# RWKV inverses and chunk steps on eight heads at a time in place of four, scores' B and K rows in separate PSUM banks, bonus product in DRAM

## Chip, cores, metric

One core of one Trainium2 chip. The metric is the device time of one execution in microseconds, median over runs. Engines: TensorE (PE), VectorE (DVE), ScalarE (ACT), SyncE (SP, which here only issues DMAs).

## What is computed

A decoder trunk of four residual layers, batch 1, 256 tokens, width 2048, all in float32: RWKV-7, dilated attention, pooling, RWKV-7. Each layer norms, projects in, mixes, gates and projects out. The change touches the two RWKV layers (32 heads of 64), whose mixer is this recurrence:

```python
def step(state, inp):                      # per head, state (64 x 64)
    r_t, w_t, k_t, v_t, a_t, b_t = inp
    sa = jnp.einsum('bhij,bhj->bhi', state, a_t)
    state = (state * w_t[:, :, None, :] + sa[..., None] * b_t[:, :, None, :]
             + v_t[..., None] * k_t[:, :, None, :])
    y_t = jnp.einsum('bhij,bhj->bhi', state, r_t)
    return state, y_t
...
y = _head_group_norm(y, lnx_w, lnx_b)
bonus = jnp.sum(heads(r * k) * r_k, axis=-1, keepdims=True) * vf
y = (y + bonus.reshape(B, S, D)) * jax.nn.silu(g)
```

## The kernel before

**Weights stream.** Every projection is `linear` (L244): 512 KB chunks of weights come by DMA on SP into `raw` (four buffers, `weights` L189), ScalarE casts them to `whi` (L196), VectorE makes the rest `wlo` (L197), and 24 matmuls `lin` per chunk (L287, 128x128 weights by 256 tokens; three products xhi·whi, xlo·whi, xhi·wlo) use it.

**The scan.** The recurrence runs in chunks of 64 tokens (four of them, `NC_`). `heads` (L675) is a generator, called eight times a layer with four heads each (`pr`; q counts two column tiles, hh the two heads in one). Its stages:

- A and S: the decays, then scores `sc` (L750): rows B and K (`BK`) against A and R (`AR`), per chunk and head 128x128; masked copies of them are `NT`, `MR` and parts of `AR`. `BT` is the transpose of `BK` (`tps` L769).
- D: the inverse of a triangular 64x64 matrix for each head and chunk. `NT` goes to DRAM and back as 16x16 blocks `Nb` on 64 partitions; 15 steps of a product and an add on VectorE (`tmp` L792, `px` L795) invert the blocks; then matmuls on 32x32 tiles (`q` L818, `zp` L834, `pp` L843) put them together to `P`.
- C: a chunk step, four times in order: `xps` (L869) from the state `SV`, its copy `X` (ACT), `ups` (L876), its copies `UV` (DVE L879, ACT L880), `sps` (L884) with the state update on VectorE (an add L887 and a product L889 per half), and the output `yps` (two groups, L894 and L897). The values of all four chunks are loaded into `SV` and `UV` at once.
- E: the epilogue: group norm sums `gps` (L909), bonus sums `bps`, norm, gate, and the store of z, which the layer's last projection reads.

**What sets the order.** `tick` (L200) is called by `linear` after every few lins. It holds the generators in a queue and draws from them; every `yield` gives the TensorE time and the delay that the step is planned with. The order of each engine is fixed when the program is built. Work of the scan so lies between lins of the same layer's projections: r, lower half of k and v, upper half of k and v, g.

A matmul of fp32 is recorded as two records in the profile.

Of the kernel before, what the change touches and what calls it, by code (L numbers as in the profile page):

```python
# [15 lines left out]
P = 128  # L16
# [79 lines left out]
class Trunk:  # L96
    def __init__(self, tc, ins, out, ctx, layers=(0, 1, 2, 3)):
# [22 lines left out]
        self.vcd = self.dp.tile([KT // 2, S, 2 * P], F32, name="vcd")  # L120
        self.ntd = [self.dp.tile([C, 2, 8, C], F32, name=f"ntd{i}") for i in range(2)]
        self.pxd = [self.dp.tile([16, 64, 32], F32, name=f"pxd{i}") for i in range(2)]

    def constants(self):
# [17 lines left out]
        n0, n1 = ix[("mu", 0, 0)], ix[("mu", 1, 5)] + 1  # L142
        self.omm = self.cp.tile([P, 12 * KT], F32, name="omm")
        nc.vector.tensor_scalar(self.omm, self.prm[:, n0 * KT:n1 * KT], -1.0, 1.0,
                                op0=ALU.mult, op1=ALU.add)
# [345 lines left out]
    def mix(self, l, m, k):  # L491
# [10 lines left out]
        for q in range(2):  # L502
# [4 lines left out]
            else:  # L507
                o = (l * 6 + m) * KT + k + q
# [73 lines left out]
    def rwkv(self, l, li):  # L582
        nc = self.nc
        a = self.i
        w2, srcs, have = {}, {}, (set(), set(), set(), set(), set(), set())
        win = lambda m: a["a_w_in"][l, m]
# [13 lines left out]
        def take_v(j, ps):  # L600
# [13 lines left out]
            def turn():  # L614

                vps = self.ps.tile([P, 2, 2, 2, C], F32, tag="ch", name="vps", bufs=2)
                for tt in range(2):
# [5 lines left out]
                nc.scalar.dma_start(  # L623
                    self.vcd[j // 2].rearrange("(t p) c -> p t c", p=P), vc)
# [50 lines left out]
    def heads(self, l, li, pr, w2, srcs, have):  # L675
# [6 lines left out]
        FLY = 3  # L682
# [7 lines left out]
        r = T("r", [P, 2, S], 1)  # L690
        dma(r, self.rd[j // 2])
# [26 lines left out]
        kp = T("kp", [P, 2, S], FLY)  # L718
        for q in range(2):
            nc.vector.scalar_tensor_tensor(kk[:, q], kt[:, q], self.col(("k_k", l), j + q),  # L720
                                           nrm[:, q], op0=ALU.mult, op1=ALU.mult)
            nc.scalar.activation(kp[:, q], aa[:, q], AF.Identity,
                                 scale=self.col(("k_a", l), j + q),
                                 bias=self.omka[:, l * KT + j + q:l * KT + j + q + 1])
        yield 0.9, 3.0
        nc.vector.tensor_tensor(kp, kp, kt, op=ALU.mult)
        BK = T("BK", [P, 2, NC_, 2, C], 1)
        AR = T("AR", [P, 2, 2, NC_, 2, C], FLY)
        for hh, rows in enumerate(half):
            nc.vector.scalar_tensor_tensor(AR[rows, hh, :, :, 0, :], c3(kk)[rows], -1.0,  # L730
                                           W[rows, :, :, 0:C], op0=ALU.mult, op1=ALU.mult)
            nc.vector.tensor_tensor(AR[rows, hh, :, :, 1, :], c3(r)[rows], W[rows, :, :, 1:],
                                    op=ALU.mult)
        nc.vector.tensor_tensor(aa, aa, kk, op=ALU.mult)
        nc.vector.tensor_tensor(BK[:, :, :, 0, :], c3(aa), c3(Wi), op=ALU.mult)
        nc.vector.tensor_tensor(BK[:, :, :, 1, :], c3(kp), c3(Wi), op=ALU.mult)
# [3 lines left out]
        yield 0.0, 5.0  # L740
# [3 lines left out]
        NT = T("NT", [P, 8, C], 2)  # L744
        MR = T("MR", [64, 2, 2, NC_, C], FLY)
        for q in range(2):
            scs = [self.ps.tile([P, NC_, 2, C], F32, tag="sm", name="sc", bufs=2) for _ in half]
            for c in range(NC_):
                for hh, rows in enumerate(half):
                    nc.tensor.matmul(scs[hh][:, c], BK[rows, q, c], AR[rows, hh, q, c],  # L750
                                     start=True, stop=True)
            yield 1.8, 2.0
            for hh, rows in enumerate(half):
                sc = scs[hh]
                nc.scalar.copy(NT[rows, q * NC_:(q + 1) * NC_], sc[0:64, :, 0, :])
                nc.vector.tensor_tensor(MR[:, q, hh], sc[0:64, :, 1, :],
                                        mk[0:64, C:].unsqueeze(1).broadcast_to([64, NC_, C]),
                                        op=ALU.mult)
                nc.vector.tensor_tensor(  # L759
                    AR[half[1 - hh], hh, q].rearrange("p c a t -> p c (a t)"),  # L760
                    sc[64:128].rearrange("p c a t -> p c (a t)"),
                    mk[64:128].unsqueeze(1).broadcast_to([64, NC_, 2 * C]), op=ALU.mult)
            yield 0.0, 1.0

        BT = T("BT", [P, 2, NC_, P], FLY)
        for q in range(2):
            tps = self.ps.tile([P, NC_, P], F32, tag="sm", name="tps", bufs=2)
# [3 lines left out]
            nc.scalar.copy(BT[:, q], tps)  # L771
        yield 0.9, 1.0

        yield "D", lambda: True
        ntd, pxd = self.ntd[pr % 2], self.pxd[pr % 2]
        for hh, rows in enumerate(half):
            dma(ntd[:, hh], NT[rows])
        Nb = T("Nb", [64, 16, 16], 1)
        for b in range(4):
            o = 16 * b  # L780
            dma(Nb[16 * b:16 * b + 16],
                ntd[o:o + 16, :, :, o:o + 16].rearrange("i h n t -> (h n) i t"))
        px = T("px", [64, 16, 2, 16], 1)
        nc.scalar.copy(px[:, :, 0], self.cst("eye16")[0:64].rearrange("p (i t) -> p i t", i=16))
        yield 0.0, 7.0
        tmp = T("tmp", [64, 64], 1)
        with self.tc.high_priority(PRIO_D):
            for i in range(15):
# [3 lines left out]
                nc.vector.tensor_tensor(t, px[:, 0:i + 1, 0, i:i + 1].broadcast_to([64, i + 1, w]),  # L792
                                        Nb[:, i:i + 1, i + 1:].broadcast_to([64, i + 1, w]),
# [3 lines left out]
        dma(pxd.rearrange("i p w -> p i w"), px.rearrange("p i w t -> p i (w t)"))  # L797
# [529 lines left out]
```

## Time and profile before

| | |
|---|---|
| median of 3 runs | 2279.78 us (2279.2 to 2280.67) |
| profiled execution | 2284.08 us, span 2282.3 us |
| PE busy | 2210.9 us (97%) |
| DVE busy | 1578.4 us (69%) |
| ACT busy | 1299.8 us (57%) |
| chain that ended last | PE 73%, DVE 13%, DMA 8%, ACT 3% |
| scans | 146 to 626 us (layer 0), 1690 to 2195 us (layer 3) |

The span is the time from the first instruction to the last on the core; the profiled execution's own time has what lies around it too. Records of matmuls overlap, so the distance from one start to the next tells more than the length of a record.

### The profile page before, as it was taken

What the parts mean: (1) busy time and instruction counts of PE and PEld (TensorE: products, weight loads), DVE (VectorE), ACT (ScalarE), POOL (GpSimd) and SP (SyncE); (2) the same over time, 40 slices, a digit from 0 to 9 for tenths busy, and PEclk for the clock granted to TensorE, in tenths of its full rate; (3) what the DMA queues carried; (4) which work ended last, traced back from release to release, by engine and by line L of the source; (5) the groups of instructions that cost most, each with busy time, mean ns of one, the idle gap of its engine ahead of it and who ended that gap; (6) DMA issues with size and microseconds to landing.
All of it is one profiled execution on the core that took longest, in us unless ns stands there. A gap on an engine that the chain in (4) does not pass through costs nothing.

```text
span 2282.3 us, 51163 instructions
## 1 busy us (share of the span) xinstructions
PE 2210.9 (97%) x21034; PEld 2025.7 (89%) x21034; DVE 1578.4 (69%) x2881; ACT 1299.8 (57%) x2050; POOL 4.7 (0%) x12
## 2 busy tenths in 40 slices
PE   7998999999999999999999999999998999999999
PEld 6998888888899888888899999998997888888989
DVE  7678788887556564656467675657677788787654
ACT  6557666665545454545466445546666666676542
POOL 0000000000000000000000000000000000000000
PEclk9999999999999999999999999999998999999999
DMA  7676777755576555355537556766585676665664
GB/s 267 224 265 184 231 216 211 215 178 173 195 245 201 186 185 194 129 177 184 193 122 257 172 182 220 249 219 228 175 296 181 209 232 202 193 200 171 204 217 154
DMA packets 217642, 464.16 MB, mean 203 GB/s; under 512 B 55488, under 2 KB 85824, under 8 KB 217408
## 3 DMA queue, kind: packets, MB, share of 16 engines
q1 hardware_dynamic: 199264, 432.92, 59.0%
q10 hardware_dynamic: 17504, 25.87, 3.3%
q8 instruction: 165, 2.70, 0.5%
q0 software_dynamic: 640, 2.10, 0.2%
q14 instruction: 69, 0.57, 0.1%
HBM read 410.47 MB, written 50.33 MB: 202 GB/s over the span
## 4 chain that ended last, share of the span: by engine, by line
PE 73%; DVE 13%; DMA 8%; ACT 3%; issue 2%; SPq 1%; DVEq 0%; POOL 0%; ACTq 0%; POOLq 0%
PE lin L287 44%; PE lin L321 17%; DMA hl<-hd 3%; DVE wlo L197 3%; PE u L542 1%; DVE xlo L173 1%; ACT whi L196 1%; DMA zl<-zd 1%; DVE mt L505 1%; PE z L567 1%; PE q L818 1%; PE yps L897 1%; DMA kt<-kd 1%; PE xps L869 1%; DVE AR L759 1%
## 5 line engine op out<-in xcount | busy, mean ns | idle before, releaser
L287 PE MATMUL lin<-xhi,whi 128*128 128x256 f32 x3584 | 1056.3, 295 | 12.3 <-ACT xhi L172 11.9
L197 DVE TENSOR_TENSOR wlo<-raw,whi 128x1024 fp32r<-128x1024 f32 x600 | 732.4, 1222 | 441.1 <-ACT whi L196 429.7
L287 PE MATMUL lin<-xlo,whi 128*128 128x256 f32 x3584 | 1024.8, 286 | 8.5 <-DVE xlo L173 8.5
L287 PE MATMUL lin<-xhi,wlo 128*128 128x256 f32 x3584 | 1022.0, 286 | 0.6 <-DVE wlo L197 0.6
L196 ACT CAST whi<-raw 128x1024 fp32r<-128x1024 f32 x600 | 627.6, 1048 | 572.0 <-PE lin L287 364.8
L287 PEld LDWEIGHTS lin<-xhi,whi 128*128 128x128 f32 x3584 | 689.0, 193 | 35.9 <-ACT xhi L172 15.0
L287 PEld LDWEIGHTS lin<-xlo,whi 128*128 128x128 f32 x3584 | 690.7, 193 | 20.1 <-DVE xlo L173 11.8
L287 PEld LDWEIGHTS lin<-xhi,wlo 128*128 128x128 f32 x3584 | 690.4, 193 | 5.0 <-issue 1.9
L321 PE MATMUL lin<-whi,xhi 128*128 128x512 f32 x576 | 229.5, 399 | 0.0
L321 PE MATMUL lin<-whi,xlo 128*128 128x512 f32 x576 | 224.6, 390 | 0.0
L321 PE MATMUL lin<-wlo,xhi 128*128 128x512 f32 x576 | 224.4, 390 | 0.0
L321 PEld LDWEIGHTS lin<-whi,xlo 128*128 128x128 f32 x576 | 108.1, 188 | 22.8
L321 PEld LDWEIGHTS lin<-wlo,xhi 128*128 128x128 f32 x576 | 108.3, 188 | 20.9
L321 PEld LDWEIGHTS lin<-whi,xhi 128*128 128x128 f32 x576 | 108.3, 188 | 20.7
L505 DVE SCALAR_TENSOR_TENSOR mt<-hl,prm 128x256 f32<-128x256 f32 x152 | 71.2, 477 | 28.2 <-DMA hl<-hd 27.1
L172 ACT CAST xhi<-mt 128x512 fp32r<-128x512 f32 x96 | 58.8, 616 | 43.4 <-DVE mt L505 37.0
L173 DVE TENSOR_TENSOR xlo<-mt,xhi 128x512 fp32r<-128x512 f32 x96 | 65.2, 683 | 5.3 <-ACT xhi L172 4.8
L509 ACT ACTIVATE mt<-H,omm 128x256 f32<-128x256 f32 x120 | 54.1, 501 | 20.9 <-PE u L542 11.3
L511 DVE SCALAR_TENSOR_TENSOR mt<-H,prm,mt 128x256 f32<-128x256 f32 x120 | 52.8, 480 | 15.7 <-ACT mt L509 14.1
L792 DVE TENSOR_TENSOR tmp<-px,Nb 64x15 f32<-64x15 f32 (+7 forms) x240 | 46.7, 194 | 5.3 <-DMA Nb<-ntd 0.7
L795 DVE TENSOR_TENSOR px<-px,tmp 64x15 f32<-64x15 f32 (+7 forms) x240 | 46.8, 195 | 4.5
L759 DVE TENSOR_TENSOR AR<-sc,c 64x512 f32<-64x512 f32 x64 | 44.4, 694 | 1.4
(228 smaller groups left out, 2222.8 us busy)
## 6 DMA issues: line engine op xcount, KB each, us to landing
raw<-in_a_w_in_dram SPq DMA_DIRECT2D x256, 512.0 KB, 4.1
raw<-in_b_qkv_dram SPq DMA_DIRECT2D x144, 512.0 KB, 3.3
hl<-hd SPq DMA_DIRECT2D x152, 256.0 KB, 4.5
raw<-in_a_w_out_dram SPq DMA_DIRECT2D x64, 512.0 KB, 4.3
raw<-in_c_w_in_dram SPq DMA_DIRECT2D x64, 512.0 KB, 3.3
raw<-in_c_w_out_dram SPq DMA_DIRECT2D x32, 512.0 KB, 3.8
raw<-in_b_gate_dram SPq DMA_DIRECT2D x16, 512.0 KB, 3.2
raw<-in_b_w_out_dram SPq DMA_DIRECT2D x16, 512.0 KB, 4.7
```

The source lines that it names most:

```text
L172: nc.scalar.copy(hi, src)
L173: nc.vector.tensor_tensor(lo, src, hi.bitcast(F32), op=ALU.subtract)
L196: nc.scalar.copy(whi, raw)
L197: nc.vector.tensor_tensor(wlo, raw, whi.bitcast(F32), op=ALU.subtract)
L287: nc.tensor.matmul(ps[:, m], a, b, start=(k == 0 and m == 0 and q == 0), stop=(k == kt - 1 and q == 2), skip_group_check=True)
L321: nc.tensor.matmul(ps, a[:, sl], b[:, kk], start=(k == 0 and q == 0), stop=(k == KT - 1 and q == 2))
L505: nc.vector.scalar_tensor_tensor(t[:, q], h[q][:, 1], mu, h[q][:, 0], op0=ALU.mult, op1=ALU.add)
L509: nc.scalar.activation(t[:, q], self.H[:, k + q, 1:], AF.Copy, scale=self.omm[:, o:o + 1])
L511: nc.vector.scalar_tensor_tensor(t[:, q], self.H[:, k + q, 0:S], mu, t[:, q], op0=ALU.mult, op1=ALU.add)
L759: nc.vector.tensor_tensor(AR[half[1 - hh], hh, q].rearrange("p c a t -> p c (a t)"), sc[64:128].rearrange("p c a t -> p c (a t)"), mk[64:1 ...
L792: nc.vector.tensor_tensor(t, px[:, 0:i + 1, 0, i:i + 1].broadcast_to([64, i + 1, w]), Nb[:, i:i + 1, i + 1:].broadcast_to([64, i + 1, w]), ...
L795: nc.vector.tensor_tensor(dst, dst, t, op=ALU.add)
```

## The change

Each `heads` call now ends after the scores and transposes and puts its tiles into a list, and every second call goes on into a new generator, `group`, with eight heads: inverse (`Nb`, `px`, `tmp`, `PX` on 128 partitions, 16 blocks), chunk steps and epilogue (the latter twice, for four heads each). Four groups a layer take the place of eight.

Scores: `sb` and `sk` are two banks; weights are the 64 columns of B or of K, on four different quarters of the array for (B, head 0), (B, head 1), (K, head 0), (K, head 1), so `MR` has 128 partitions. Transposes become matmuls with a 64x64 identity, into quarters.

Values: `SV` and `UV` are loaded for one chunk at a time (two buffers each, four DMAs a chunk), from a store that ScalarE's queue writes in two DMAs rather than one. The bonus product `kp` is stored to DRAM (`bd`) and loaded in the epilogue. r is loaded later, into the buffer of `kt`. `raw` has three buffers, not four. `AR`, `MR`, `BT` and `Wc` have four, not three; the vector `omm` (1 - mu) is made per layer. Flags in `st` keep one user of `BK`, `NT` and `Y` at a time, and let a `heads` call start only when the group before the last has ended its chunks.

```diff
@@ __init__, weights
-        self.vcd = self.dp.tile([KT // 2, S, 2 * P], F32, name="vcd")
+        self.bd_ = self.dp.tile([KT // 2, P, 2, S], F32, name="bd")
+        self.vcd = self.dp.tile([KT // 4, S, 2, 2, 2, C], F32, name="vcd")
-        raw = self.wp.tile([P, k, nb], F32, tag="raw", name="raw", bufs=4)
+        raw = self.wp.tile([P, k, nb], F32, tag="raw", name="raw", bufs=3)
@@ heads: four heads a call
-        kp = T("kp", [P, 2, S], FLY)
+        kp = T("kp", [P, 2, S], 1)
...
+        while st["BK"]:
+            yield 0.0, 1.0
+        st["BK"] = True
+        r = T("kt", [P, 2, S], 1)
+        dma(r, self.rd[j // 2])
...
+        dma(self.bd_[j // 2], kp)
...
-            scs = [self.ps.tile([P, NC_, 2, C], F32, tag="sm", name="sc", bufs=2) for _ in half]
+            sb, sk = (self.ps.tile([P, NC_, 2, C], F32, tag="sm", name="sc", bufs=2)
+                      for _ in range(2))
             for c in range(NC_):
                 for hh, rows in enumerate(half):
-                    nc.tensor.matmul(scs[hh][:, c], BK[rows, q, c], AR[rows, hh, q, c],
+                    nc.tensor.matmul(sb[rows, c], BK[rows, q, c, 0], AR[rows, hh, q, c],
+                                     start=True, stop=True)
+                for hh, rows in enumerate(half):
+                    nc.tensor.matmul(sk[half[1 - hh], c], BK[rows, q, c, 1], AR[rows, hh, q, c],
                                      start=True, stop=True)
...
-                nc.tensor.transpose(tps[:, c], BK[:, q, c].rearrange("p b t -> p (b t)"),
-                                    self.cst("ident"))
+                for b in range(2):
+                    for hh, rows in enumerate(half):
+                        nc.tensor.matmul(tps[hh][half[hh ^ b], q, c], BK[rows, q, c, b],
+                                         idn[rows, rows], start=True, stop=True)
...
+        st["BK"] = False
+        grp.append((AR, MR, BT, Wc))
+        if pr % 2:
+            yield from self.group(l, li, pr // 2, have, grp, st)
+
+    def group(self, l, li, gr, have, grp, st):
...
-        for n in range(8):
+        for n in range(16):
...
+        def values(c):
+            SV = T("SV", [P, 2, 2, 2, C], 2)
+            UV = T("UV", [P, 2, 2, 2, C], 2)
+            vc = vv[c * C:(c + 1) * C]
+            for hh, rows in enumerate((half[1], half[0])):
+                for t in (SV, UV):
+                    dma(flat(t[rows, hh]), flat(vc[:, hh]))
+            return SV, UV
...
-            for q, hh, rows in each:
-                nc.tensor.matmul(xps[rows, q], AR[:, hh, q, c, 0, :], SV[:, c, hh, q, :],
+            xps = bank("xps")
+            for s, q, hh, rows in each:
+                nc.tensor.matmul(xps[rows, q, s], grp[s][0][:, hh, q, c, 0, :], SV[:, hh, q, s],
                                  start=True, stop=True)
+            nxt = values(c + 1) if c < NC_ - 1 else None
...
-                    nc.vector.tensor_tensor(SV[rows, c + 1, hh], SV[rows, c, hh], sps[rows],
-                                            op=ALU.add)
-                    nc.vector.tensor_tensor(SV[rows, c + 1, hh], SV[rows, c + 1, hh],
-                                            Wc[rows, :, c:c + 1].broadcast_to([64, 2, C]),
-                                            op=ALU.mult)
+                    S_ = nxt[0][rows, hh]
+                    nc.vector.tensor_tensor(S_, SV[rows, hh], sps[rows], op=ALU.add)
+                    for s in range(2):
+                        nc.vector.tensor_tensor(
+                            S_[:, :, s], S_[:, :, s],
+                            grp[s][3][rows, :, c:c + 1].broadcast_to([64, 2, C]), op=ALU.mult)
...
+            dma(kp, self.bd_[j // 2])
```


The inverse's steps keep their form at twice the size, and `zp`, `pp`, `ups`, `sps`, `yps` follow the pattern of `xps`.

**TensorE, a score set in layer 0.** Names are out<-moving,weights and each tile's number; a row with x2 is two alike. Before:

```order
L750 MATMUL sc_4605<-AR_4369,BK_4368 128x128
L750 MATMUL sc_4606<-AR_4369,BK_4368 128x128
L750 MATMUL sc_4605<-AR_4369,BK_4368 128x128
L750 MATMUL sc_4606<-AR_4369,BK_4368 128x128
L750 MATMUL sc_4605<-AR_4369,BK_4368 128x128
L750 MATMUL sc_4606<-AR_4369,BK_4368 128x128
L750 MATMUL sc_4605<-AR_4369,BK_4368 128x128
L750 MATMUL sc_4606<-AR_4369,BK_4368 128x128
L876 MATMUL ups_4617<-X_4615,P_4558 64x64 x4
L287 MATMUL lin_4525<-xhi_3629,whi_4467 128x256
```

Of the change, at a set of the same layer (L771 is B, L774 is K; L920 is `xps`, L284 is `lin`):

```order
L284 MATMUL lin_4647<-xhi_4673,wlo_4583 128x256
L771 MATMUL sc_5053<-AR_4360,BK_4359 64x128 x2
L774 MATMUL sc_5054<-AR_4360,BK_4359 64x128 x2
L771 MATMUL sc_5053<-AR_4360,BK_4359 64x128 x2
L774 MATMUL sc_5054<-AR_4360,BK_4359 64x128 x2
L771 MATMUL sc_5053<-AR_4360,BK_4359 64x128 x2
L774 MATMUL sc_5054<-AR_4360,BK_4359 64x128 x2
L284 MATMUL lin_4647<-xhi_4770,whi_4582 128x256
L771 MATMUL sc_5053<-AR_4360,BK_4359 64x128 x2
L774 MATMUL sc_5054<-AR_4360,BK_4359 64x128 x2
L920 MATMUL xps_5159<-SV_5151,AR_2721 64x64 x4
```

Eight matmuls of 128x128 have become eight of B and eight of K, in pairs; here a lin stands among them, and `xps` of a group follows in the same run.

**TensorE, a chunk step near the end of layer 0's scan.** Before, from `sps` to the next `xps`:

```order
L884 MATMUL sps_8606<-UV_8448,BT_7331 64x64 x4
L287 MATMUL lin_8709<-xhi_8346,wlo_8482 128x256
L287 MATMUL lin_8709<-xhi_8372,whi_8481 128x256
L287 MATMUL lin_8709<-xlo_8373,whi_8481 128x256
L287 MATMUL lin_8709<-xhi_8372,wlo_8482 128x256
L287 MATMUL lin_8709<-xhi_8372,whi_8481 128x256
L894 MATMUL yps_8615<-AR_6761,SV_8449 64x64 x4
L897 MATMUL yps_8615<-MR_7089,UV_8448 64x64 x4
L287 MATMUL lin_8709<-xlo_8373,whi_8481 128x256
L287 MATMUL lin_8709<-xhi_8372,wlo_8482 128x256
L287 MATMUL lin_8709<-xhi_8372,whi_8481 128x256
L869 MATMUL xps_8625<-SV_8449,AR_6761 64x64 x4
```

Of the change (L936 `sps`, L947 and L950 `yps`):

```order
L936 MATMUL sps_8371<-UV_8293,BT_6985 64x64 x4
L936 MATMUL sps_8371<-UV_8293,BT_7459 64x64 x4
L947 MATMUL yps_8386<-AR_6033,SV_8292 64x64 x4
L947 MATMUL yps_8386<-AR_7111,SV_8292 64x64 x4
L950 MATMUL yps_8386<-MR_6718,UV_8293 64x64 x4
L950 MATMUL yps_8386<-MR_7242,UV_8293 64x64 x4
L284 MATMUL lin_8616<-xhi_8103,whi_8252 128x256
L920 MATMUL xps_8404<-SV_8309,AR_6033 64x64
L284 MATMUL lin_8616<-xlo_8104,whi_8252 128x256
L284 MATMUL lin_8616<-xhi_8103,wlo_8253 128x256
L920 MATMUL xps_8404<-SV_8309,AR_6033 64x64 x3
L920 MATMUL xps_8404<-SV_8309,AR_7111 64x64 x4
```

The step has twice the matmuls, for two sets of tiles (two numbers of `BT`, `AR`, `MR`); `sps` and `yps` stand together, and three lins lie between `yps` and the end of the next `xps`.

**VectorE, the same stretch.** Before, the state updates (L887, L889) and the copies `UV`, without the tiles' numbers:

```order
L879 COPY UV<-ups 64x128
L887 TENSOR_TENSOR SV<-SV,sps 64x128 x2
L889 TENSOR_TENSOR SV<-SV,Wc 64x128 x2
L197 TENSOR_TENSOR wlo<-raw,whi 128x1024
L925 TENSOR_TENSOR Y<-Y,gl 128x512
L173 TENSOR_TENSOR xlo<-zl,xhi 128x512 x2
L879 COPY UV<-ups 64x128
L173 TENSOR_TENSOR xlo<-zl,xhi 128x512
L197 TENSOR_TENSOR wlo<-raw,whi 128x1024
L887 TENSOR_TENSOR SV<-SV,sps 64x128 x2
L889 TENSOR_TENSOR SV<-SV,Wc 64x128 x2
```

Of the change (L940, L942, L931):

```order
L931 COPY UV<-ups 64x256
L940 TENSOR_TENSOR SV<-SV,sps 64x256 x2
L942 TENSOR_TENSOR SV<-SV,Wc 64x2x64 x4
L194 TENSOR_TENSOR wlo<-raw,whi 128x1024
L636 TENSOR_TENSOR gs<-gs,lin 128x512
L931 COPY UV<-ups 64x256
L940 TENSOR_TENSOR SV<-SV,sps 64x256 x2
L942 TENSOR_TENSOR SV<-SV,Wc 64x2x64 x4
L194 TENSOR_TENSOR wlo<-raw,whi 128x1024
L931 COPY UV<-ups 64x256
L940 TENSOR_TENSOR SV<-SV,sps 64x256 x2
L942 TENSOR_TENSOR SV<-SV,Wc 64x2x64 x4
```

An update was four operations of 128 elements a row; it is two of 256 and four of 2x64 a row (that is 128), for twice the heads, and there are half as many updates.

## Rows read from the trace of the kernel before

**Rows 1.** Windows of both scans, summed; columns: engine and its busy us.

```profile
sum 985.00, PE 942.32 PEld 834.90 DVE 766.88 ACT 642.84 POOL 0.00; mean PE 471.16 PEld 417.45 DVE 383.44 ACT 321.42 POOL 0.00
```

**Rows 2.** Same windows, `lin` alone: window, us, PE busy (count), granted clock, DMA share, GB/s.

```profile
146.00:626.00 480.00, 321.37 (x2280) 0.99 0.66 204
1690.00:2195.00 505.00, 332.32 (x2295) 0.97 0.64 201
```

**Rows 3.** TensorE timeline in layer 0: start us, us, then line, tile, shapes, records.

```profile
562.16 0.28 PE L287 MATMUL lin<-xhi,wlo 128*128 128x256 f32 x1
562.37 0.45 PE L869 MATMUL xps<-SV,AR 128*64 128x64 f32 x8
...
562.97 0.28 PE L287 MATMUL lin<-xlo,whi 128*128 128x256 f32 x1
...
565.10 0.45 PE L876 MATMUL ups<-X,P 64*64 64x64 f32 x8
...
565.70 0.28 PE L287 MATMUL lin<-xlo,whi 128*128 128x256 f32 x1
...
567.62 0.28 PE L287 MATMUL lin<-xhi,wlo 128*128 128x256 f32 x1
...
568.44 0.45 PE L897 MATMUL yps<-MR,UV 64*64 64x64 f32 x8
...
569.04 0.28 PE L287 MATMUL lin<-xlo,whi 128*128 128x256 f32 x1
569.16 0.28 PE L287 MATMUL lin<-xhi,wlo 128*128 128x256 f32 x1
```

**Rows 4.** TensorE timeline, a score set in layer 0.

```profile
178.30 0.28 PE L287 MATMUL lin<-xhi,wlo 128*128 128x256 f32 x1
178.51 1.16 PE L750 MATMUL sc<-AR,BK 64*128 64x128 f32 x16
...
179.82 0.28 PE L287 MATMUL lin<-xlo,whi 128*128 128x256 f32 x1
```

**Rows 5.** TensorE timeline, transposes and inverse in layer 0.

```profile
436.97 1.03 PE L769 MATMUL tps<-c,BK 128*128 128x128 f32 x8
...
437.96 0.28 PE L287 MATMUL lin<-xlo,whi 128*128 128x256 f32 x1
...
438.43 0.28 PE L287 MATMUL lin<-xhi,wlo 128*128 128x256 f32 x1
438.64 0.72 PE L818 MATMUL q<-Z,PX 32*32 32x32 f32 x62
...
440.11 0.28 PE L287 MATMUL lin<-xlo,whi 128*128 128x256 f32 x1
```

**Rows 6.** Groups by form, VectorE: state update and masks (busy us, mean ns; idle before).

```profile
L889 DVE TENSOR_TENSOR SV<-SV,Wc 64x128 f32<-64x128 f32 x96 | 27.4, 286 | 2.7
L887 DVE TENSOR_TENSOR SV<-SV,sps 64x128 f32<-64x128 f32 x96 | 27.3, 284 | 18.7 <-PE sps L884 16.7
L756 DVE TENSOR_TENSOR MR<-sc,c 64x256 f32<-64x256 f32 x64 | 26.5, 415 | 9.5 <-ACT NT L755 8.2
```

**Rows 7.** Page part 5: the rest of the weights, and the inverse's products.

```profile
L197 DVE TENSOR_TENSOR wlo<-raw,whi 128x1024 fp32r<-128x1024 f32 x600 | 732.4, 1222 | 441.1 <-ACT whi L196 429.7
...
L792 DVE TENSOR_TENSOR tmp<-px,Nb 64x15 f32<-64x15 f32 (+7 forms) x240 | 46.7, 194 | 5.3 <-DMA Nb<-ntd 0.7
```

**Rows 8.** Waits of TensorE: for what, us in total, times, longest us.

```profile
PE xps L869 <- DVE SV L889: 2.2, 6, 0.4
```

**Rows 9.** TensorE timeline at the end of layer 0's scan.

```profile
625.53 1.04 PE L909 MATMUL gps<-gsq,c 128*128 128x512 f32 x2
...
636.51 0.51 PE L287 MATMUL lin<-xhi,whi 128*128 128x256 f32 x2
```

**Rows 10.** Waits of SyncE's queue.

```profile
SPq L193 <- DVE wlo L197: 1109.7, 473, 8.5
```

**Rows 11.** DMA issues: tile, engine, count, KB each, median us to landing.

```profile
SV<-vcd SPq DMA_DIRECT2D x32, 128.0 KB, 3.7
```

More of the change, by code (lines that the diff above doesn't have):

```diff
@@ L827, in heads @@
         pp = prod(lambda o, n: Z[:, n], P0, 32)
-        yield 2.6, 2.0
+        yield 2.6, 2.5
         nc.vector.tensor_tensor(X0, X0, xp, op=ALU.add)
         nc.vector.tensor_tensor(P0, P0, pp, op=ALU.add)
-        zp = self.ps.tile([P, 8, 32], F32, tag="nt", name="zp", bufs=2)
-        for n in range(8):
+        zp = bank("zp")
+        for n in range(16):
             for b in (0, 64):
@@ L835, in heads @@
                                  start=True, stop=True)
[L836 to L837 removed]
+        st["NT"] = None
+        yield 1.0, 2.0
+        Z2 = T("px", [P, 16, 32], 1)
         for b in (0, 64):
             nc.scalar.copy(Z2[b + 32:b + 64], zp[b + 32:b + 64])
[L840 to L841 removed]
+        pp = bank("pp")
+        for n in range(16):
             for b in (0, 64):
@@ L844, in heads @@
                                  start=True, stop=True)
-        Pm = T("P", [P, 8, C], 2)
+        yield 1.0, 1.5
+        yield "C", lambda: (4 * gr in have[2] and 4 * gr + 2 in have[2] and not st["Y"])
+        Pm = T("P", [P, 16, C], 1)
         for o in range(2):
@@ L861, in heads @@
+        each = [(s, q, hh, rows) for s in range(2) for q in range(2)
+                for hh, rows in enumerate(half)]
+        SV, UV = values(0)
         for hh, rows in enumerate(half):
-            nc.vector.memset(SV[rows, 0, hh], 0.0)
-        Y = T("Y", [P, 2, S], 1)
-        each = [(q, hh, rows) for q in range(2) for hh, rows in enumerate(half)]
+            nc.vector.memset(SV[rows, hh], 0.0)
+        bank = lambda name: self.ps.tile([P, 2, 2, C], F32, tag="ch", name=name, bufs=2)
         for c in range(NC_):
-            xps = self.ps.tile([P, 2, C], F32, tag="ch", name="xps", bufs=2)
-            for q, hh, rows in each:
-                nc.tensor.matmul(xps[rows, q], AR[:, hh, q, c, 0, :], SV[:, c, hh, q, :],
+            xps = bank("xps")
+            for s, q, hh, rows in each:
+                nc.tensor.matmul(xps[rows, q, s], grp[s][0][:, hh, q, c, 0, :], SV[:, hh, q, s],
@@ L870, in heads @@
                                  start=True, stop=True)
-            yield 0.44, 1.3
-            X = T("X", [P, 2, C], 2)
+            nxt = values(c + 1) if c < NC_ - 1 else None
+            yield 0.5, 1.3
+            X = T("X", [P, 2, 2, C], 1)
             nc.scalar.copy(X, xps)
-            ups = self.ps.tile([P, 2, C], F32, tag="ch", name="ups", bufs=2)
-            for q, hh, rows in each:
-                nc.tensor.matmul(ups[rows, q], Pm[rows, q * NC_ + c], X[rows, q],
-                                 start=True, stop=True)
@@ L892, in heads @@
-            yps = self.ps.tile([P, 2, C], F32, tag="ch", name="yps", bufs=2)
-            for q, hh, rows in each:
-                nc.tensor.matmul(yps[rows, q], SV[:, c, hh, q, :], AR[:, hh, q, c, 1, :],
-                                 start=(q == 0), stop=False, skip_group_check=True)
-            for q, hh, rows in each:
-                nc.tensor.matmul(yps[rows, q], UV[0:64, c, hh, q, :], MR[:, q, hh, c, :],
-                                 start=False, stop=True, skip_group_check=True)
@@ L899, in heads @@
-            yield 1.21, 1.3
-            nc.scalar.copy(Y[:, :, c * C:(c + 1) * C], yps)
+            ups = bank("ups")
+            for s, q, hh, rows in each:
+                nc.tensor.matmul(ups[rows, q, s], Pm[rows, s * 8 + q * NC_ + c],
+                                 X[rows, q, s], start=True, stop=True)
+            yield 0.4, 1.6
+            nc.vector.tensor_copy(UV[0:64, 0], ups[0:64])
+            nc.scalar.copy(UV[64:128, 1], ups[64:128])
+            if nxt:
+                sps = bank("sps")
+                for s, q, hh, rows in each:
+                    nc.tensor.matmul(sps[rows, q, s], grp[s][2][:, hh, q, c],
+                                     UV[:, hh, q, s], start=True, stop=True)
+                for hh, rows in enumerate(half):
+                    S_ = nxt[0][rows, hh]
[4 more added lines that the diff above has]
+                            grp[s][3][rows, :, c:c + 1].broadcast_to([64, 2, C]), op=ALU.mult)
@@ new lines, in group @@
+            yps = bank("yps")
+            for s, q, hh, rows in each:
+                nc.tensor.matmul(yps[rows, q, s], SV[:, hh, q, s], grp[s][0][:, hh, q, c, 1, :],
+                                 start=(s == 0 and q == 0), stop=False, skip_group_check=True)
+            for s, q, hh, rows in each:
+                nc.tensor.matmul(yps[rows, q, s], UV[rows, hh, q, s], grp[s][1][rows, q, c],
+                                 start=False, stop=True, skip_group_check=True)
+            yield 1.6, 1.5
```

201 lines of the change are left out of this document (106 added, 95 removed).

## Prediction

> **What bounds the kernel now.** I read the page first (its busy shares), then the two stretches in which the changed code runs: the scans of layer 0 (146 to 626 us) and of layer 3 (1690 to 2195 us), by windows of engine time. Of their 985.0 us TensorE is busy for 942.3 and VectorE for 766.9 [rows 1]; idle time of TensorE is 42.7 us. So in both scans the time is TensorE's stream, in its own order, and VectorE is second with some room. The same windows for the tile `lin` alone count 2280 and 2295 instructions, at a granted clock of 0.99 and 0.97 (nearly all of the time the upper level, 2.4 GHz) [rows 2]. A lin that follows a lin starts 0.12 us after it (569.04 and 569.16 in [rows 3]; all plain stretches read so), so they take 4575 x 0.12 = 549 us of the 985. The other 436 us are small matmuls put between lins, and waits. Idle time is only 43 of them. What the change can save is therefore what a small matmul adds to TensorE's stream, not what it is busy for (records overlap); I read that from start to start.
>
> Between the last lin before a piece of small work and the second lin behind it lie two lin pitches, 0.24 us, and the rest was added. For the eight records of xps (four matmuls of fp32, two records each, 64 columns a record): 562.97 - 562.16 - 0.24 = 0.57 us [rows 3]. For the sixteen of sc, 128 columns each: 179.82 - 178.30 - 0.24 = 1.28 us [rows 4]. The first are 512 columns and the second 2048, so a column costs 0.71 / 1536 = 0.46 ns and what is left, 0.33 us, is paid for entering and leaving tiled matmuls once, whatever their number. I call that a **run**. The run sps, yps, yps at the end of a chunk step adds 569.04 - 567.62 - 0.24 = 1.18 us [rows 3]: 0.33 + 3 x 0.24 leaves 0.14, and in it the tile changes once, from 128*64 to 64*64. So a **change of tile inside a run** is 0.14 us. The inverse's q, 128 records of 32 columns on 32*32 tiles, adds 440.11 - 438.43 - 0.24 = 1.44 us [rows 5]; less 0.33 that is 0.27 ns a column against 0.46: the four tiles on the array's diagonal work at once, where xps and sc have two.
>
> **The change part by part.** *Fewer runs.* Columns of the inverse and of the chunk steps stay as they are, since eight heads need twice the columns of four in half as many runs. I counted runs (tiled matmuls between two lins) and changes of tile inside them in TensorE's order of the whole program: runs 274 before and 185 after, changes 124 and 53. That gives 89 x 0.33 = -29 us and 71 x 0.14 = -10 us.
>
> *Scores.* A set had 16 records of 128 columns on two row halves of the array; it now has 32 on 64*64 tiles, B and K apart. No row of before has four 64*64 tiles at once. Bounds: at the two-at-a-time price of rows 3 and 4, 4096 x 0.46 = 1.89 us a set, 0.95 more than now, times 32 sets = +30 us; at half that price, nothing. I take nothing, since in the order the four tiles of a chunk follow each other (two of B, two of K) and lie in four different quarters of the array, and q shows four tiles at work. Four of the 32 sets have their B and K rows drawn apart by the scheduler and then only pairs can meet: 4 x 0.9 = +4 us.
> The Trainium skill (TensorEngine Tiling (Array Packing), Gotcha 1: PSUM Pressure) says that different row tiles cannot access the same PSUM bank simultaneously; by it, B's two matmuls, which lie in one bank on different rows, would take turns, as would K's, and the sum would come out as the first rival's below. The trace differs: the runs ups and yps<-MR do that now, and 565.70 - 565.10 for ups is no longer than 562.97 - 562.37 for xps, 0.60 us each [rows 3].
>
> *Transposes.* A call's eight records of 128 columns run in the lins' own tile and add 437.96 - 436.97 - 0.12 = 0.87 us [rows 5], 14 us for 16 calls. Now they are 64 records of 64 columns, four at a time 4096 x 0.23 = 0.94 us, 15 us (their runs are counted above): +1. Two at a time: +15 more.
>
> *State update.* VectorE did two adds of 284 ns and two products of 286 ns, 1.14 us, between sps and the next xps; now two adds of 256 elements, for which the 415 ns of the like operation MR<-sc stands, and four products of 286 [rows 6]: 1.97 us. In 17 of the 24 chunk steps followed by another, far more lins than that stand between and hide it. In seven, at the layers' tails, two to five lins do (0.24 to 0.6 us). There yps gives 2 x 0.47 + 0.14 of cover, so 1.97 and some 0.2 for the hand-over less 1.3 to 1.7 is 0.5 to 0.9 us of waiting; a wlo of 1.22 us [rows 7] stands in VectorE's order at some of them, which makes at most 2.1. Bounds 7 x 0.5 = 3 to 7 x 2.1 = 15; I take 7 x 1.3 = 9. Now this wait is six times, 2.2 us in all [rows 8]. What is queued behind xps then is the lins of the layer's last part, so it is time on the path. Four of the eight inverses also have q, q and zp with no lin between, at the 0.3 us of such a hand-over: +1.
>
> *Tail.* The last epilogue now makes two z blocks after each other; 11 us pass from gps to the lin that reads the block (625.53 to 636.51) [rows 9], and 62 to 83 lins (7 to 10 us) stand there in the order, 76 and 83 before: +2, between 0 and 6.
>
> *VectorE's relief.* The 240 products of the inverse, at 194 ns, and its 240 adds, taken at the same, become half as many: -47 us [rows 7]. Masks (MR) halve from 64 x 415 ns: -13. The update falls from 96 x 570 ns to 24 x 1.97 us: -7 [rows 6]. That is 67 of 767 us, 9%. If TensorE's 42.7 us of waits fall by as much, -4; bounds 0 and -21 (half of them).
>
> *Edits at nothing.* One raw buffer less: the weight loads would have 2.9 us less to be ahead by, where a chunk of 24 lins takes 24 x 0.12. Of a load's waits for its buffer the typical is 1109.7 / 473 = 2.3 us on SyncE behind VectorE's wlo [rows 10], with the cast still far ahead of the lins; if that cover went, each late chunk would cost up to 2.9 us, and 20 of them 58. The bonus product's store and reload (16 of 256 KB each way), the values' store in two transfers in place of one, the later load of r and the flags lie tens of us ahead of their readers. Chunk loads: the second rival.
>
> Sum: -29 - 10 + 4 + 1 + 9 + 1 + 2 - 4 = **-26 us**. The profiled execution took 2284.1, 4.3 above the median of the runs shown, so 2258 on its scale and **2254 us** against the median. 0.2% is 4.6 us, about what a measurement here can tell from no change.
>
> **The rivals.** *Tiles in pairs (slower).* If four 64*64 tiles don't work at once, scores cost +30 and transposes +15: -26 + 45 = +19, or 2299 us; if only the scores are hit, +4, 2284. For it: no row shows four. Against it: q, and ups in one bank. The kernel is slower by over 0.2% from 0.23 + 0.23 x (26 + 4.6) / 45 = 0.39 ns a column.
>
> *Chunk loads late (slower).* SV and UV come per chunk now, 24 times behind the first, each time four transfers issued on SyncE behind weight loads that wait. A transfer lands after 3.7 us [rows 11], and the wait ahead of it is 2.3 us in the mean, 8.5 at the longest [rows 10]: 6.0 to 12.2 us. A chunk step has at least 6.7 us from its xps to the next where lins are plenty (562.37 to beyond 569.04 [rows 3]), less in the seven tail steps. It makes the kernel slower by over 0.2% from a mean wait of (26 + 4.6) / 24 = 1.3 us a load; at 2 us it is +48 - 26 = +22, 2302 us. Against it: the issue stands a whole step ahead, and a wait there is only what those two numbers leave over.
>
> *Waits halve (faster still).* Half as many inverses and chains mean half as many hand-overs: -21 in place of -4, **2237 us**. Against it: many of the 43 us belong to norms, mixes and the lora products, which stay.
>
> **How the numbers follow.** Forecast 0.66 (own range 2240 to 2270, from the bounds of update, tail and relief), waits halve 0.08, pairs 0.13 (0.01 faster, 0.04 same, 0.08 slower), late loads 0.10 (slower), something unforeseen 0.03 (0.02 the same, 0.01 slower). Faster 0.66 + 0.08 + 0.01 = 0.75, same 0.06, slower 0.19. The range runs from 2230 (below the third rival) to 2282, which leaves out the late loads and most of the pairs.
>
> **What the profile of the changed kernel would show.** Runs: xps with sixteen records adding 0.33 + 0.47 = 0.80 us from lin to lin; 1.14, twice the 0.57 of now, says that the price of a run grows with its records, and then the 29 us are not there. Scores: 32 records adding 1.3 us (four at a time) or 2.2 (pairs). Transposes: 64 records adding 1.3 or 2.2. Waits of xps for SV's products at the tails, about 9 us in all; for SV's loads, under 1. If waits of lin for wlo or whi appear in the scans, the raw buffer was not free.

## The result, and the profile after

The changed kernel takes **2317.24 us** (median) against 2280.23 for the kernel before, a ratio of 1.0157 (95% interval 1.0137 to 1.0177): slower by 37 us, where 26 us faster had been forecast. One of the four executions behind the median took 10449 us at a granted clock of 0.184; the ratio leaves it out. The profiled execution took 2314.95 us, 30.9 more than that of before.

The changed kernel's page, the rows on the span, on TensorE and on its granted clock in 40 slices:

```profile
span 2313.2 us, 53463 instructions
...
PE 2194.3 (95%) x22442; PEld 2026.7 (88%) x22442; DVE 1510.2 (65%) x2482; ACT 1257.2 (54%) x1850; POOL 4.6 (0%) x12
...
PEclk9999898989999999999999999999999999999999
```

TensorE is busy for 16.6 us less than before (2210.9) and the span is 30.9 us longer. The clock falls in the slices of the first scan. The windows of rows 1, for the changed kernel:

```profile
sum 985.00, PE 896.74 PEld 817.36 DVE 689.10 ACT 589.80 POOL 0.00; mean PE 448.37 PEld 408.68 DVE 344.55 ACT 294.90 POOL 0.00
```

and those of rows 2, `lin` alone (window, us, PE busy and count, granted clock, DMA share, GB/s):

```profile
146.00:626.00 480.00, 304.55 (x2211) 0.94 0.66 205
1690.00:2195.00 505.00, 334.53 (x2414) 0.95 0.69 214
```

VectorE did get the forecast relief (on the whole page 1510.2 us in place of 1578.4, -68; forecast -67). But TensorE is idle for 985.0 - 896.7 = 88 us in place of 43, and the granted clock is 0.94 and 0.95 in place of 0.99 and 0.97 [rows 1, 2]. The windows hold the same times, not quite the same work: the last gps of the two scans now begin at 648.5 and 2224.8 us, behind the windows' ends.

The prices of single runs, from TensorE's timeline in layer 0 (start us, us):

```profile
181.80 0.28 PE L284 MATMUL lin<-xhi,wlo 128*128 128x256 f32 x1
182.01 0.33 PE L771 MATMUL sc<-AR,BK 64*64 64x128 f32 x2
...
183.26 0.28 PE L284 MATMUL lin<-xlo,whi 128*128 128x256 f32 x1
...
311.59 0.28 PE L284 MATMUL lin<-xhi,wlo 128*128 128x256 f32 x1
311.80 0.69 PE L920 MATMUL xps<-SV,AR 128*64 128x64 f32 x16
...
312.64 0.28 PE L284 MATMUL lin<-xlo,whi 128*128 128x256 f32 x1
...
519.64 0.28 PE L284 MATMUL lin<-xhi,wlo 128*128 128x256 f32 x1
519.85 0.69 PE L936 MATMUL sps<-UV,BT 128*64 128x64 f32 x16
...
521.77 0.28 PE L284 MATMUL lin<-xlo,whi 128*128 128x256 f32 x1
```

As in the prediction, from the last lin before to the second behind, less 0.24: a set of scores adds 183.26 - 181.80 - 0.24 = 1.22 us (forecast 1.3 with four tiles at once, 2.2 in pairs), xps 312.64 - 311.59 - 0.24 = 0.81 (0.80), sps with both yps 521.77 - 519.64 - 0.24 = 1.89 (0.33 + 3 x 0.47 + 0.14 = 1.88). The price list was right to 0.1 us. The loss is in the waits of TensorE (us in total, times, longest):

```profile
PE q L860 <- issue: 44.0, 16, 4.0
PE lin L284 <- ACT xhi L169: 23.5, 15, 5.8
...
PE bps L972 <- DMA kb<-bd: 6.9, 5, 2.1
...
PE lin L284 <- DVE xlo L170: 5.8, 12, 1.3
...
PE zp L876 <- issue: 2.7, 2, 1.7
```

In the kernel before the first row was:

```profile
PE q L818 <- issue: 2.8, 3, 2.2
```

Now it is 44.0 us in 16, two in each of the eight inverses. "Issue" is time in which TensorE waited for nothing that the profile shows. Taken together, the rows of this view rose from 66.2 to 114.2 us: +41 for issue, +9 for DMAs (kb above all), -2 for everything else. One inverse in the timeline:

```profile
257.29 1.29 PE L860 MATMUL q<-PX,NT 16*32 16x32 f32 x128
...
259.65 0.43 PE L771 MATMUL sc<-AR,BK 64*64 64x128 f32 x2
261.20 0.62 PE L860 MATMUL q<-px,PX 32*32 32x32 f32 x49 [1.12 <-ACT px L867]
264.05 1.27 PE L860 MATMUL q<-px,PX 32*32 32x32 f32 x77 [2.23 <-issue]
...
269.97 1.12 PE L860 MATMUL q<-PX,px 32*32 32x32 f32 x68 [4.00 <-issue]
...
273.42 0.64 PE L876 MATMUL zp<-PX,NT 32*32 32x32 f32 x15 [1.00 <-issue]
...
276.28 0.41 PE L284 MATMUL lin<-xlo,whi 128*128 128x256 f32 x1
276.49 0.41 PE L284 MATMUL lin<-xhi,wlo 128*128 128x256 f32 x1
```

The two products q (L860, 256 records) begin at 261.20 and go on past 270; 2 x 1.11 = 2.2 us follow from the prediction's price for 128 records. They stand still twice, for 2.23 and 4.00 us, and again in zp. The lins behind run at 276.49 - 276.28 = 0.21 us each, not at 0.12. The windows say why (us, PE busy and count, granted clock, DMA share, GB/s):

```profile
258.00:262.00 4.00, 2.70 (x127) 1.00 1.03 333
262.00:266.00 4.00, 1.93 (x128) 0.72 0.80 255
266.00:270.00 4.00, 0.03 (x4) 0.50 0.91 314
270.00:274.00 4.00, 3.00 (x145) 0.50 0.46 156
274.00:278.00 4.00, 4.00 (x45) 0.58 0.30 108
278.00:282.00 4.00, 4.00 (x89) 1.00 0.47 159
```

The granted clock falls from 262 on, where TensorE stood still for 2.23 us, and from 266 to 274 us it is 0.50, the lower level of 1.2 GHz; in the first half of that TensorE did next to nothing (0.03 us). So a stall costs twice: its own length, and some microseconds at half speed behind it.

What does it wait for? The page's row of the instruction queue (packets, MB, share of 16 engines):

```profile
q8 instruction: 176, 2.88, 0.5%
```

and that of the kernel before:

```profile
q8 instruction: 165, 2.70, 0.5%
```

22442 matmuls and as many weight loads of TensorE are 44884 instructions; 2.88 MB are 64 bytes for each, and in the kernel before 2.70 MB for 42068, again 64. So this queue brings TensorE's own instructions, in packets of 16.4 KB, which is 256 instructions or 128 records of matmul with their weight loads. The same queue in the window 267.3 to 268.5 us, inside the second stall:

```profile
q8 instruction: 1, 0.02, 5.0%
```

One packet came there, none in 266.0 to 267.3 nor in 268.5 to 270.0, and TensorE went on at 269.97. That suggested that it had run out of instructions; the experiments test it.

All stalls of the eight inverses read so, the 16 at q and the two at zp behind it: each ends 2.2 to 2.8 us after a packet of this queue has begun. The first stall of an inverse comes after 14 to 112 of its 256 records, so at no fixed place of the products, and the next one exactly 128 records behind it, which is one packet (77 + 1 + 2 + 48 between the two shown, with the short rows that are left out). Other DMA traffic is not needed for a stall. In the one at zp that ends at 392.16 us no transfer began (columns as above):

```profile
390.47:392.16 1.69, 0.00 (x1) 0.50 0.00 0
```

In others the DMA share was up to 0.98; whether traffic makes a stall longer was not separated.

### The profile page after: what moved, and what is told of

Read it like the earlier page. It is cut to its first block, busy times and chain, and to the rows that moved or that the text cites. A ratio compares the mean times of both kernels' runs of the same rounds, so it can differ in the third digit from the quotient of the medians.

```text
span 2313.2 us, 53463 instructions
## 1 busy us (share of the span) xinstructions
PE 2194.3 (95%) x22442; PEld 2026.7 (88%) x22442; DVE 1510.2 (65%) x2482; ACT 1257.2 (54%) x1850; POOL 4.6 (0%) x12
## 3 DMA queue, kind: packets, MB, share of 16 engines
q8 instruction: 176, 2.88, 0.5%
## 4 chain that ended last, share of the span: by engine, by line
PE 79%; DMA 8%; DVE 6%; issue 4%; ACT 3%; SPq 0%; ACTq 0%; POOL 0%; DVEq 0%; POOLq 0%
PE lin L284 47%; PE lin L318 17%; DMA hl<-hd 3%; DVE wlo L194 2%; PE u L539 1%; PE q L860 1%; DMA kb<-bd 1%; DMA raw<-in_a_w_in_dram 1%; PE z L564 1%; ACT whi L193 1%; PE sc L771 1%; PE yps L950 1%; DVE xlo L170 1%; PE xps L920 1%; DVE mt L502 1%
## 5 line engine op out<-in xcount | busy, mean ns | idle before, releaser
L284 PE MATMUL lin<-xhi,whi 128*128 128x256 f32 x3584 | 1054.8, 295 | 23.9 <-ACT xhi L169 23.5
L284 PE MATMUL lin<-xlo,whi 128*128 128x256 f32 x3584 | 1030.2, 288 | 6.1 <-DVE xlo L170 5.8
L284 PE MATMUL lin<-xhi,wlo 128*128 128x256 f32 x3584 | 1026.1, 287 | 0.9 <-DVE wlo L194 0.9
L284 PEld LDWEIGHTS lin<-xhi,whi 128*128 128x128 f32 x3584 | 694.4, 194 | 47.9 <-ACT xhi L169 27.2
L284 PEld LDWEIGHTS lin<-xlo,whi 128*128 128x128 f32 x3584 | 696.0, 194 | 20.9 <-DVE xlo L170 9.6
L284 PEld LDWEIGHTS lin<-xhi,wlo 128*128 128x128 f32 x3584 | 695.5, 194 | 5.3 <-issue 2.4
L539 PE MATMUL u<-l,mt 128*128 128x96 f32 (+1 forms) x320 | 42.3, 269 | 0.0
L771 PE MATMUL sc<-AR,BK 64*64 64x128 f32 x512 | 42.2, 289 | 0.1
```

What stands on the lines that cost most here:

```text
L284: nc.tensor.matmul(ps[:, m], a, b, start=(k == 0 and m == 0 and q == 0), stop=(k == kt - 1 and q == 2), skip_group_check=True)
L539: nc.tensor.matmul(u[:, tt], x[:, q, tt * P:(tt + 1) * P], wt[:, k + q], start=(k + q + tt == 0), stop=(k + q == KT - 1), skip_group_check ...
L771: nc.tensor.matmul(sb[rows, c], BK[rows, q, c, 0], AR[rows, hh, q, c], start=True, stop=True)
```

## Experiments

Theory **instructions run dry**: a burst of 256 short records takes 512 instructions in some 2 us, two packets, faster than packets come (inside the inverses they begin 3.4 to 6.1 us apart). Rivals: a **hidden wait** of the products themselves (a buffer, a hand-over), the **clock** as the main loss, and **the steps on eight heads** with their loads.

**The products in pieces of 64 records.**

```diff
-        yield 0.0, 14.0
+        yield 0.0, (18.0 if gr < KT // 4 - 1 else 14.0)
...
+            for m in range(2):
+                for n in range(8 * m, 8 * m + 8):
...
+                yield 0.9, (2.5 if gr < KT // 4 - 1 else 0.0)
...
```

> The changed kernel with the inverse's products q drawn in pieces of 64 records; lins lie between the pieces in six of the eight inverses (12 to 24 lins, 1.4 to 2.9 us), and in the last inverse of each layer all of qN, q, zp and pp now follow each other without a lin. Theory 'instructions run dry' (TensorE uses its instructions faster than new ones arrive when a long burst of short matmuls stands together): idle of q without a visible cause falls from 44.0 us to near 0 in the six, and grows in the two last ones, where 512 records stand in one burst, from about 6 to 10 us each; sum 15 to 25 us, and the time falls from 2317 to 2280 to 2300. Rival 'hidden wait' (the idle belongs to the products themselves, some buffer or hand-over that the profile doesn't show): two stalls in each inverse wherever it is cut, 44 us as now, and 24 more runs of 0.33 us: 2325. Rival 'clock' (the loss is mostly the lower clock): idle falls with the bursts, but the time hardly does, 2310 or more.

```profile
PE q L861 <- ACT PX L850: 20.7, 2, 11.4
...
PE q L861 <- issue: 5.1, 6, 1.8
```

2342.69 us (1.0277, 1.0250 to 1.0304). The idle did go (5.1 us), which speaks against the hidden wait, but the time rose. The growth that was expected in the two last inverses did not come: at q they stall for 2.0 and 2.2 us, at a granted clock of 0.50, where 128 records take 1.7 us in place of 1.1. The first row shows where the time went: the longer plan put the last group of each layer behind the last lin. In the timeline its inverse, steps and epilogue make one stretch of 62.6 us without a lin, twice. The experiment moved two things at once, and its time decides nothing.

**A break between the two products only.**

```diff
...
+                yield 0.3 + 1.1 / pieces, wait
...
-        xp = prod(lambda o, n: P0[:, n], Z, 32)
-        pp = prod(lambda o, n: Z[:, n], P0, 32)
-        yield 2.6, 2.5
+        xp = yield from prod(lambda o, n: P0[:, n], Z, 32, 1, 2.0)
+        pp = yield from prod(lambda o, n: Z[:, n], P0, 32, 1, 2.0)
```

> The changed kernel with a break between the two products of q only, so pieces of 128 records; 4 to 18 lins (0.5 to 2.2 us) lie between them in five inverses, none in the first and in the last of each layer. 'Instructions run dry': the stall in the middle becomes shorter by what the lins between give, so idle of q without a visible cause is 20 to 36 us, and the time 2295 to 2310. 'Hidden wait': 44 us, 2317 to 2322.

```profile
PE q L861 <- issue: 31.5, 16, 4.1
```

31.5 us, as expected of a break of half a microsecond to two; but 2335.25 us (1.0235, 1.0208 to 1.0262), and here too the delays in the plan (4 us also behind qN) pushed the last group back: at the ends of the two scans stand stretches of 25 and 34 us without a lin. That the time was missed for this reason is likely, not tested.

**The kernel before with each product issued twice.**

```diff
-                    nc.tensor.matmul(q_[o:o + 32, n], fa(o, n)[o:o + kk_], fb[o:o + kk_, n],
-                                     start=True, stop=True)
+                    for _ in range(2 if kk_ == 32 else 1):
+                        nc.tensor.matmul(q_[o:o + 32, n], fa(o, n)[o:o + kk_],
+                                         fb[o:o + kk_, n], start=True, stop=True)
```

> The kernel before with each matmul of the two products q issued twice (the second writes the same values again), so that its run of q has 256 records in place of 128, as in the change, with nothing else of the change. 'Instructions run dry': idle of q without a visible cause, 2.8 us in the kernel before, becomes 3 to 6 us in each of the 16 inverses, and the time 2280 + 18 for the records + 48 to 96 for the stalls + 15 to 25 for the clock behind them: 2360 to 2410. 'Hidden wait' in the change's own 16 block form: no stalls, 2280 + 18 = 2298.

```profile
PE q L819 <- issue: 38.9, 15, 4.5
...
PE lin L287 <- issue: 6.8, 3, 3.6
```

2349.53 us (one run). Nothing of the change is here but the length of the burst, and the stalls come: 15 at q, in 14 of the 16 inverses, and three at lins right behind q, two of them in the other two inverses. Their sum, 45.7 us, is just below the expected 48 to 96, and so is the time, but it is 51 us above the 2298 of the rival. The hidden wait, a matter of the change's own form, falls.

**Scores with B's eight matmuls ahead of K's.**

```diff
             for c in range(NC_):
                 for hh, rows in enumerate(half):
                     nc.tensor.matmul(sb[rows, c], BK[rows, q, c, 0], AR[rows, hh, q, c],
                                      start=True, stop=True)
+            for c in range(NC_):
                 for hh, rows in enumerate(half):
                     nc.tensor.matmul(sk[half[1 - hh], c], BK[rows, q, c, 1], AR[rows, hh, q, c],
```

> The changed kernel with the eight matmuls of B ahead of the eight of K in each score set, so that only two 64*64 tiles can work side by side. If four at once is what makes a set's 32 records add 1.23 us: 2.0 to 2.2 us now, 32 sets x 0.8 to 0.95 = +26 to +30, 2343 to 2347. If the price of a record doesn't hang on its neighbours: 1.23 us and 2317.

```profile
180.65 0.28 PE L284 MATMUL lin<-xhi,wlo 128*128 128x256 f32 x1
180.86 0.76 PE L771 MATMUL sc<-AR,BK 64*64 64x128 f32 x10
...
182.60 0.28 PE L284 MATMUL lin<-xlo,whi 128*128 128x256 f32 x1
```

A set adds 182.60 - 180.65 - 0.24 = 1.71 us in place of 1.22: the neighbours matter, but by 0.49 us, about half of what was expected. That B and K still meet in the middle of a set (181.36 to 181.73 in the same timeline has records of both) can be one reason. Over 32 sets that is 16 us, and yet the time is 2318.36 (one run) against 2317.24. In the profiled executions TensorE is busy for 12.1 us more (2206.4 against 2194.3) and waits for 8.4 us less (105.8 against 114.2, of which 6 at q): smaller waits hide most of the price. Why they are smaller is open.

**Inverses on four heads, chunk steps on eight.** The inverse of the kernel before stands again in `heads`.

```diff
-            st["NT"] = T("NT", [P, 16, C], 1)
+        NT = T("NT", [P, 8, C], 2)
...
+        PX = T("PX", [P, 8, 2, 32], 1)
...
+        grp.append((AR, MR, BT, Wc, Pm))
```

> The change without its first half: inverses take four heads at a time as in the kernel before (8 blocks on 64 partitions, q in runs of 128 records, NT in two buffers), chunk steps take eight; scores, chunk loads, bonus product in DRAM and raw's three buffers are those of the change. 'Instructions run dry': idle of q without a visible cause falls from 44.0 us to under 8, and all other terms of the sum stay: 2317 less 44 for the stalls, less about 13 for the clock behind them, plus 8 more inverses x 4 runs x 0.33 = 11 us, is 2271 (2260 to 2282), faster than the kernel before. Rival 'chunk loads and the new waits': the loss comes with the steps on eight heads, their loads and the bonus product, which stay here: 2305 or more.

```profile
PE lin L284 <- ACT xhi L169: 20.6, 10, 5.8
...
PE lin L284 <- DVE xlo L170: 10.5, 14, 2.2
...
PE q L841 <- issue: 5.0, 4, 2.2
```

2304.35 us (1.0105, 1.0085 to 1.0125). The stalls are gone (5.0 us), but of the expected 46 us only 13 came; measured stands beside the rival's 2305. Bursts of instructions are not the whole loss. The waits of lin for xhi and xlo are 31 us (20 before), and all waits together 88.8 against 66.2. Against the change they fell by 25 us in all, not by the 39 of the stalls, and TensorE is busy for 10 us longer (2204.6 against 2194.3), about the 11 that the added runs had been costed at.

**The bonus product loaded earlier**, in that kernel:

```diff
+            if c == NC_ - 1:
+                for s in range(2):
+                    kp = self.mp.tile([P, 2, S], F32, tag="io", name="kb", bufs=4)
+                    dma(kp, self.bd_[2 * gr + s])
...
```

> The kernel of inverses on four and chunk steps on eight heads, with the loads of the bonus product issued ahead of the last chunk step in place of the epilogue. The wait of bps for kb, 6.9 us in the changed kernel, falls to under 1 and the time by 4 to 7 us against the same kernel without it (2265 by the first theory); if the reload is hidden anyway, no difference.

```profile
PE yps L946 <- ACT UV L928: 6.0, 1, 6.0
```

The wait for kb is gone (3.8 us without the edit), and the kernel is slower all the same: 2311.41 us (1.0140, 1.0120 to 1.0159). An expectation missed. TensorE's waits are 8.1 us more (96.9 against 88.8), most of that the one shown: ScalarE came late with UV because it had stood still for 7.4 us for a load of kt, which SyncE had issued behind kb's two. That kb's loads delayed it is read from one execution and was not tested.

**Three raw buffers in the kernel before** (`bufs=4` to `bufs=3`, nothing else).

> The kernel before with three raw buffers in place of four and nothing else. As costed in the prediction: nothing, 2280 (within 5 us). If the fourth buffer covers the weight stream's jitter: waits of lin for wlo or whi appear, and 10 us or more.

2275.22 us, ratio 0.9981 (0.9969 to 0.9992): as costed, nothing is lost, and a little gained. The fastest kernel of this study.

**NT for four heads, in three buffers.** In the change one NT for eight heads holds back the next group's scores until the inverse has read it.

```diff
-            st["NT"] = T("NT", [P, 16, C], 1)
+        NT = T("NT", [P, 8, C], 3)
...
-        Nb = T("Nb", [P, 16, 16], 1)
+        PX = T("PX", [P, 16, 2, 32], 1)
+        flat_ = PX.rearrange("p n w t -> p (n w t)")
+        Nb = flat_[:, 256:512].rearrange("p (a b) -> p a b", b=16)
...
-        tmp = T("tmp", [P, 64], 1)
+        tmp = flat_[:, 0:64]
```

> The changed kernel with NT as a tile for four heads in three buffers in place of one tile for eight heads in one (room for it by keeping tmp and Nb inside PX), so that the next group's scores don't wait until the inverse has read NT; the products q stay in one burst of 256 records, and the order now has the last group's steps well ahead of the last lins. 'Instructions run dry': idle of q without a visible cause stays at 35 to 45 us, the time within 15 us of the changed kernel's, 2302 to 2317. If the loss was the late last group: 2285 or less.

```profile
PE q L857 <- issue: 35.4, 14, 4.8
```

2302.56 us (1.0095, 1.0071 to 1.0120): 15 us better than the change, with 35.4 us of stalls left. The last q of layer 0 comes at 555 us in place of 605, so the last group did move; the late group was not the main loss, for which 2285 or less had been expected.

**The same, and the products in pieces of 64 records** (`yield 0.9, 1.5` behind each piece, 1.0 for qN, 16 in place of 14 ahead of them). This is the first pair in which the last group stays well ahead of the last lins on both sides. The delays in the plan, and with them the order around the inverses, still differ a little.

> The same with the products q in pieces of 64 records with 12 to 36 lins between them in nearly all inverses, and the last group still ahead of the last lins, as it was not in the first kernel with pieces. 'Instructions run dry': idle of q without a visible cause under 8 us, clock time at the lower level down by 30 to 60 us, 24 to 32 more runs (+10): 2317 - 38 - 20 + 10 = 2269 (2255 to 2282). If the new waits of other engines make up the rest, as in the kernel with inverses on four heads: 2285 to 2305.

```profile
PE lin L284 <- ACT xhi L169: 22.2, 12, 5.8
...
PE q L858 <- issue: 5.2, 4, 3.5
PE ssp L717 <- DVE MR L773: 4.9, 2, 4.5
...
PE bps L968 <- DMA kb<-bd: 1.2, 2, 0.7
```

2278.49 us (0.9993, 0.9976 to 1.0009), 24.1 us less than without pieces, inside the expected 2255 to 2282 and level with the kernel before. The granted clock of the whole span is 0.986; it was 0.976 without pieces, and 0.973 in the change.

**The same with longer breaks.**

> The same with longer planned breaks (18 us ahead of the products and 2.5 us between pieces in place of 16 and 1.0 to 1.5), so that no two pieces stand together, but the last group comes about 100 lins later. Idle of q without a visible cause under 4 us; the time within 8 us of the one with shorter breaks, above it if the place of the last group matters.

```profile
PE q L858 <- issue: 0.4, 1, 0.4
```

No stalls, but 2288.89 us (1.0041, 1.0022 to 1.0060), 10 more than with short breaks. The expectation put such a loss down to the place of the last group, and the waits do not show it: they are 8.7 us less in all (77.4 against 86.1). TensorE is busy for 23 us more (2212.1 against 2189.0). Its order has 22 more runs, 7 us at the price of a run (an estimate), and the granted clock of 0.983 in place of 0.986 is 7 us of the span. The rest is open.

## Why the prediction was wrong

**The step that failed** is *Fewer runs*: columns "stay as they are", so 89 runs less are 89 x 0.33 us. The prices hold (0.81, 1.22 and 1.89 us against 0.80, 1.3 and 1.88), and no term asked how many instructions a run takes. A run of q with 256 records is the one where that decides: 44.0 us of idle that was nowhere in the sum, and the lower clock behind it. The row for it was there: the kernel before had 2.8 us of issue at q in three stalls, in runs of half the length, and rows 5 show 128 records in 1.1 us. Shown by the runs on both sides: the kernel before with longer bursts gets the stalls (38.9 us), and pieces take them away (35.4 to 5.2 us) and with them 24.1 us of time, although TensorE's order then has 43 runs with q in place of 16. That stalls lie 128 records apart, a packet's worth, says the same.

The Trainium skill (Runtime: NRT & Kernel Launch, Instruction fetch mechanics) says that each engine's instructions come in 16 KiB blocks of 256 and that the cost of crossing a block's end is mostly hidden. The first half agrees with the 16.4 KB of a packet here; the second holds for lins (none of the changed kernel waits for issue), but not where 256 records of 8.7 ns stand together: 16 stalls, up to 4.0 us each.

**Tail**, forecast at +2: the late last group cost at most some 15 us (the change against its copy with three NT buffers). Not all of that need be the tail: the copy has 9 us less of stalls too, and the two profiled executions differ by 5.9 us (2313.2 and 2307.3). The prediction saw the lins behind gps, but not that one NT for eight heads makes each group's scores wait for the inverse ahead. That is the buffer the grouping itself doubled in size.

**The sum's other terms.** Of the 30.9 us more in the profiled executions, +48 are waits, so all the rest is -17, and in it lies the clock: 1 - 0.973 of 2313.2 us against 1 - 0.988 of 2282.3 is 35 us more lost, part of it while TensorE was idle anyway. The runs and changes so gave between -17 and -52; the prediction had -34 (-29 - 10 + 4 + 1). With the stalls and the late group repaired, the span is 2.4 us below that of before, +20 of waits, +5 of clock, and so -27 of runs, where the forecast with 27 more runs is -25. The transposes hold as well: 64 records add 456.39 - 454.86 - 0.24 = 1.29 us (1.3). The state update, +9, cost no wait: none of xps for SV stands in the changed kernel's list. VectorE's relief came (-68), but bought next to nothing: the waits that are neither issue nor DMA fell by 2.

**The rivals.** Tiles in pairs: no, 1.22 us a set. That B's two row tiles write into one bank does not keep four tiles from working. Loads of chunks late: no wait of xps for its loads in the list; kb, which had been costed at nothing, waited 6.9 us in five places. Waits halve: they rose from 66.2 to 114.2 us. The raw buffer: lin waits for wlo and whi for 1.3 us in all (0.6 before), so it was free, as the run with three buffers says. The clock as the main loss: it is at most 35 us beside 41 more of issue, and it came back with the stalls (0.976 to 0.986); no run separates the two. None of the rivals was the one that came; slower had a chance of 0.19, of which 0.01 for something unforeseen.

**Open.** Level with before, the repaired kernel is still some 24 us above the forecast. By the sums above 12 are waits (+20, where the sum had 9 + 1 + 2 - 4 = +8), 7 are runs (-27 in place of -34, for its pieces) and 5 the clock. The waits are those of lin for xhi (22.2 us; the row of before stands below), of ssp (12 against 5) and for DMAs (5, where before had 0.2).

```profile
PE lin L287 <- ACT xhi L172: 11.9, 5, 5.8
```

Which of the change's parts makes them was not separated. Of the 63 us between forecast and result, 24 so belong to the bursts, 15 to the single NT buffer with what it moves, and 24 have no tested cause.

## To carry to other kernels

Count instructions as well as columns: merging runs saves their fixed price, but a long burst of very short matmuls can use instructions faster than they arrive, and each stall then also costs the clock. Look for idle time with no cause in the profile of the kernel before, in the same kind of burst, and put long work between pieces of some 64 records. When a tile is doubled, look at how many buffers it has left: the serial order that this makes can show at the end of the stage.

## What the hardware showed that was not expected

TensorE's instructions are a stream of 64 bytes each, in packets of 16.4 KB on a DMA queue of their own, and a burst of 256 fp32 records on 32x32 tiles, 8.7 ns each, outruns it: stalls of up to 4.8 us, 128 records apart, each over 2.2 to 2.8 us after a packet begins in the changed kernel. Four 64x64 tiles, in four quarters of the array and two banks, take 32 records of 128 columns in 1.22 - 0.33 = 0.89 us, 28 ns a record. One raw buffer less made the kernel before faster by 0.2%.
